# Regrouped PSUM sums, a stage-wide matmul order and one more pair in two stages of a trunk kernel

## The chip, the cores and the metric

The kernel runs on one core of a Trainium2 chip. The metric is the device time in microseconds, the median of several runs. The engines are TensorE (PE, with weight loads shown as PEld), VectorE (DVE), ScalarE (ACT), GpSimd (POOL) and SyncE (SP), which here only issues transfers.

## The reference

One layer of a streaming encoder on 1024 tokens of width 1024, all in float32:

```
h = rmsnorm(x) ; u = h @ w_in            # columns for three mixers, and 3 x 1024 gate columns
y_hg, y_ml, y_mb = HGRN2, mLSTM and Mamba-2 scans over chunks of u
gates = sigmoid(gate columns)
mixed = sum_b gates[b] * (y_b @ w_br_b) ; x = x + mixed @ w_out
u = conv3(rmsnorm(x) @ w_up) ; x = x + (silu(u_g) * u_v) @ w_down      # 2 x 2816 up columns
out = rmsnorm(x)
```

The change touches two projections: the 24 blocks of 128 gate columns, and the 44 blocks of 128 up columns, taken in 22 twos f (a block of u_g and the block of u_v beside it).

## The kernel before

Activations lie transposed: 128 channels on the partitions, 1024 tokens along the free axis. Every float32 operand is split into a high part (a cast to the matmul's format, ACT, L99) and a low part (the remainder, DVE, L100), and a product is hi\*hi + hi\*lo + lo\*hi. A plain block of 128 columns is thus 8 pieces of the contraction x 3 products x 2 token halves = 48 matmuls of 128x512 (`steps`, L136), and two blocks are 96.

Most gate and up blocks are done two at a time, with seven half-size products instead of eight (`pair_gemm` and `seven`): the contraction is halved, the tokens are halved, and some operands are sums or differences. Each of the seven is 12 matmuls (`product`, L171), so a pair is 84. Four PSUM sums take part. x is written four times, always adding to what it holds; y, z and v once each. The order is x, y, x, z, x, v, x. After each of the first three writings of x, ACT copies it out (`keep`, L188); DVE adds y, z and v to these copies (`add`, L183); at the end ACT copies x once more (L192).

PSUM has two pools. `pg` has two buffers of 1024 floats per partition (two banks each), named ps_g; `pm` has four of 512 floats, named ps_m. A plain block uses one ps_g. Before the change a pair has x and y as the two halves of one ps_g, and z and v in two ps_m. A tile is the unit on which the framework sets dependences and hands out buffers.

A pair's weights are prepared in `operands`: two raw blocks are loaded by SP (four buffers, w_raw, shared with all other weights and with the branches' y tiles), split into wa (the first block), qb (named w_b), and, after four differences in place on DVE (L160), s12 and s34 (named w_s). wa and s12 use the two buffers w_hi and w_lo that plain weights use too. This work has a higher priority with the planner than its place in the program.

The token side, `sums`, makes four differences t1 to t4 of quarters of the activations (DVE, L221) and splits them (L99, L100), once at the start of each of the two stages. The pool `a1`, which holds a pair's w_b, w_s, c and u, is opened where the sums' inputs lay, so its first use waits until these have been read.

The order of instructions on each engine is found at build time by a planner that simulates the program and takes, per engine, the ready instruction with the highest priority. `manual_schedule` fixes the written order of the named engines inside its block; instructions of other blocks can still come between. Before the change each pair is a block of its own.

The two stages: four plain gates (GATES), then the `sums`, eight gate pairs (blocks 4 to 19), four plain gates (20 to 23), and the branches, which load, cast and split the eight y tiles of a mixer (L870) and multiply. Later, f=0 of the up projection, plain f=1 and f=2 (range(1, PLAIN)), during which the `sums` are made on DVE and ACT, and 19 pairs f=3 to 21; each pair is followed by two convolutions (`up_conv`, L601 and L605), a SiLU and a product (L958, L959), and a store. Then the down projection: its first group needs two stored activations, and x2, which is fetched into the place that the t tiles leave (L241), and adds on DVE (L1001).

Of the kernel before, what the change touches and what calls it, by code (L numbers as in the profile page):

```python
# [9 lines left out]
F32 = mybir.dt.float32  # L10
# [8 lines left out]
P = 128  # L19
# [3 lines left out]
HALF = 512  # L23
# [24 lines left out]
class Trunk:  # L48
# [125 lines left out]
    def pair_gemm(self, pool, srcs, outs):  # L174

        nc = self.nc
        wa, s12, s34, qb = self.operands(pool, srcs)
        ps = self.pg.tile([P, T], F32, name="ps_g")
        x, y = ps[:, 0:HALF], ps[:, HALF:]
        z, v = (self.pm.tile([P, HALF], F32, name="ps_m") for _ in range(2))  # L180
        oa, ob = outs
        tmp = lambda: pool.tile([P, HALF], F32, name="u", bufs=4)
        add = lambda out, p, q: nc.vector.tensor_tensor(out=out, in0=p, in1=q, op=ALU.add)  # L183
        u = []

        def keep():
            u.append(tmp())
            nc.scalar.copy(out=u[-1], in_=x)  # L188

        with self.tc.manual_schedule(engines={mybir.EngineType.PE}):  # L190
            self.seven(wa, s12, s34, qb, (x, y, z, v), u, keep, add, oa, ob)
        nc.scalar.copy(out=ob[:, 0:HALF], in_=x)  # L192

    def seven(self, wa, s12, s34, qb, banks, u, keep, add, oa, ob):
        b11, b21, b22, t1, t2, t3, t4 = self.bs
# [645 lines left out]
            self.keep(self.gate_d[i], g)  # L841

    def gate_pairs(self, pool, some):
        for i in some:
            cs = [pool.tile([P, T], F32, name="c", bufs=3) for _ in range(2)]
            self.pair_gemm(pool, [self.ins["w_gate"][i + j] for j in range(2)], cs)
            for j in range(2):
                self.gate_end(i + j, cs[j])
# [120 lines left out]
            self.act(f, us)  # L969

    def up_pairs(self, pool, fs):
        for f in fs:
            ns = (2 * f, 2 * f + 1)
            cs = [pool.tile([P, T], F32, name="c", bufs=3) for _ in ns]
            self.pair_gemm(pool, [self.ins["w_up"][n] for n in ns], cs)
            us = []
            for n, c in zip(ns, cs):
                us.append(self.gp.tile([P, T], F32, name="gate", bufs=3))
                self.up_conv(us[-1], c, n)
            self.act(f, us)  # L980
# [49 lines left out]


GATES = 4
PLAIN = 3
FF_GROUPS = [(0, 2)] + [(4 * g + 2, 4) for g in range(5)]


# [106 lines left out]
def build(tc, ins, outs, dbg=None):  # L1143
    stages = dbg or dict(hg=8, ml=4, mb=4, rest=True)
    left = dict(side="left", reuse_waits="tile")
    right = dict(side="right", reuse_waits="tile")
    with ExitStack() as ctx:
        t = Trunk(tc, ctx, ins, outs, dbg)
        t.y_dram = [outs[f"y{i}"] for i in range(3)] if dbg else [
            t.dr.tile([KT, P, T], F32, name=f"y_dram{i}") for i in range(3)]  # L1150
        t.h_d = t.dr.tile([2, P, KT, HALF], F32, name="h_dram")
        t.gate_d = t.dr.tile([24, P, T], F32, name="gate_dram")
        t.x2_d = t.dr.tile([KT, P, T], F32, name="x2_dram")
        t.act_d = t.dr.tile([22, P, T], F32, name="act_dram")
        with tc.tile_pool(name="gp", bufs=3, **right) as t.gp:
            with tc.tile_pool(name="hp", bufs=1, **right) as hp:
                with ExitStack() as ms:
                    late = ms.enter_context(tc.tile_pool(name="late", bufs=1, **right))
                    early = lambda: Mix(ms.enter_context(tc.tile_pool(name="early", bufs=1, **right)), late)
                    mp, begun, v = t.first(hp, early)  # L1160
                    t.late_consts(late)
                    t.hg_setup()
                    for hd in range(stages["hg"]):
                        if hd and hd % 2 == 0:
                            v = t.hg_v(mp, hd // 2)
                        t.hg_head(mp, hd, v, begun if hd == 0 else None)
                        if hd == 5:
                            t.scalars(mp)
                    for hd in range(stages["ml"]):
                        t.ml_head(mp, hd)  # L1170
                    for g in range(stages["mb"]):
                        t.mb_group(mp, g)
                if not stages["rest"]:
                    return
                t.gates(range(GATES))
                with tc.tile_pool(name="tp", bufs=1, **right) as tp:
                    with tc.tile_pool(name="hx", bufs=2, **left) as hx:
                        xs = [hx.tile([P, KT, HALF], F32, name="h_x") for _ in range(2)]
                        for ks, hf in itertools.product((slice(0, KT // 2), slice(KT // 2, KT)), range(2)):
                            t.fetch(xs[hf][:, ks], t.h_d[hf][:, ks])  # L1180
                        quarter = lambda hf, k0: [[t.h[hf][part][:, k0 + k] for k in range(KT // 2)] for part in range(2)]
                        t.bs = [quarter(0, 0), quarter(0, KT // 2), quarter(1, KT // 2)] + t.sums(tp, xs)
                    with tc.tile_pool(name="a1", bufs=1, **left) as pool:
                        t.gate_pairs(pool, range(GATES, 24 - GATES, 2))
                t.gates(range(24 - GATES, 24))
                yp = ctx.enter_context(tc.tile_pool(name="yp", bufs=KT, **left))
                xps = ExitStack()
                xp = xps.enter_context(tc.tile_pool(name="x2", bufs=2, **left))
                br = t.branches(yp, xp)
                mixed = next(br)  # L1190
            with tc.tile_pool(name="mx", bufs=KT, **right) as mxp:
                mix = [t.pair(mxp, mixed[j]) for j in range(KT - 2)]
                for _ in br:
                    pass
                mix += [t.pair(mxp, mixed[j]) for j in range(KT - 2, KT)]
                x2 = [xp.tile([P, KT, HALF], F32, name="x2") for _ in range(2)]

                hs = [[[], []] for _ in range(4)]
                for n, part, e in itertools.product((1, 0, 2, 3), range(2), ("p_hi", "p_lo")):
                    w = yp.tile([P, T], F32R, name=e, align_bytes=ALIGN, bufs=KT)  # L1200
                    hs[n][e == "p_lo"] += [w[:, 0:HALF], w[:, HALF:]]
                place = lambda part, kt, hf: hs[kt // 4 * 2 + hf][part][kt % 4]
                rhs = lambda part, kt, ts: place(part, kt, ts.start // HALF)
                tmp = t.halves_of(lambda: t.gp.tile([P, T], F32, name="gate", bufs=3))
                src = [lambda kt, hf=hf: x2[hf][:, kt] for hf in range(2)]
                sums = lambda hf: t.norm_sums(tmp, src[hf], slice(0, HALF))


                def norm2(dg, hf):
                    t.norm(src[hf], dg, src[hf], "norm2_g",  # L1210
                           lambda kt, a: t.split(place(0, kt, hf), place(1, kt, hf), a))
                t.out_proj(mix, x2, 0, range(KT))
                t.out_proj(mix, x2, 1, [0])
                dg = sums(0)
                t.out_proj(mix, x2, 1, [1])
                norm2(dg, 0)
                t.out_proj(mix, x2, 1, range(2, KT))
            begun = t.up_begin(rhs)
            dg = sums(1)
            with tc.tile_pool(name="tp", bufs=1, **right) as tp:  # L1220
                ws, done = t.up_end(*begun, lambda: norm2(dg, 1))
                t.up_plain(range(1, PLAIN), rhs, ws)
                with tc.issue_after(done.ins):
                    t.bs = [hs[0], hs[2], hs[3]] + t.sums(tp, x2)
                xps.close()
                with tc.tile_pool(name="a1", bufs=1, **left) as pool:
                    t.up_pairs(pool, range(PLAIN, 22))
            with tc.tile_pool(name="dn", bufs=1, **right) as pool:
                t.down(yp, pool)
# [15 lines left out]
```

## Time and profile before

| | us |
|---|---|
| median of 3 runs (2536.49 to 2537.75) | 2537.37 |
| the profiled execution: its own time | 2535.01 |
| its span, first to last instruction | 2533.2 |

The span is what the profile shows. Its rows give, for a group of instructions, the busy time, the count and the mean length; a bracket at the end of a row gives the idle time of the engine before it and what ended that. A matmul's length (0.39 us) holds its way through the array, and the next starts before it ends, so distances between starts tell the pace. With a mean granted clock of 0.995 the core ran almost all of the span at the full clock. DVE was busy for 59% of the span and ACT for 40%.

### The profile page before, as it was taken

To read this page: it belongs to the slowest core of one execution; us is meant where nothing else is said; L and a number is where in the kernel's file an instruction comes from. 1 tells how busy PE (TensorE), PEld (TensorE's weight loads), DVE (VectorE), ACT (ScalarE), POOL (GpSimd) and SP (SyncE) were. 2 spreads that over 40 slices of the span, in tenths; PEclk is the share of its full clock that TensorE was granted. 3 is DMA by queue.
4 is the path that set the end of the run, shared out by engine and by line. 5 is a ranking of instruction groups with operands and counts; after the bars stand their busy time and mean duration, and the time that the engine had idled before them with its cause. 6 is when DMAs were issued, how large, how long until landed. Compare 5 with 4: busy or idle time off the path is not lost.

```text
span 2533.2 us, 31151 instructions
## 1 busy us (share of the span) xinstructions
PE 2474.8 (98%) x12980; PEld 2111.6 (83%) x12980; DVE 1503.5 (59%) x1888; ACT 1003.5 (40%) x1233; POOL 62.2 (2%) x99
## 2 busy tenths in 40 slices
PE   8999999999999999999999999999999999999998
PEld 6898989898898898899877888888777777778886
DVE  6676767774344366766844324444687777775445
ACT  5444445553334255446433312212344444441112
POOL 2000000000000000000000000000000000000000
PEclk8999999999999999999999999999999999999999
DMA  5111111111111122122323444444222222244321
GB/s 215 34 41 44 42 42 34 53 59 58 67 67 60 49 92 80 61 69 92 150 100 105 162 134 156 156 135 150 100 76 82 75 75 77 82 136 147 108 75 67
DMA packets 64141, 228.63 MB, mean 90 GB/s; under 512 B 7400, under 2 KB 8040, under 8 KB 63232
## 3 DMA queue, kind: packets, MB, share of 16 engines
q1 hardware_dynamic: 52352, 181.54, 21.6%
q0 software_dynamic: 11648, 45.09, 4.5%
q8 instruction: 102, 1.67, 0.3%
q14 instruction: 39, 0.32, 0.0%
HBM read 177.23 MB, written 49.38 MB: 89 GB/s over the span
## 4 chain that ended last, share of the span: by engine, by line
PE 94%; DVE 2%; ACT 2%; issue 1%; DMA 1%; POOL 0%; DVEq 0%; ACTq 0%
PE ps_g L136 48%; PE ps_g L171 14%; PE ps_g L270 10%; PE ps_m L171 6%; PE ps_m L136 5%; PE ps_m L464 3%; PE ps_m L797 1%; ACT w_hi L99 1%; PE ps_m L270 1%; PE ps_m L473 1%; PE ps_m L708 1%; PE ps_m L679 1%; PE ps_m L483 1%; PE ps_m L436 0%; PE ps_m L659 0%
## 5 line engine op out<-in xcount | busy, mean ns | idle before, releaser
L136 PE MATMUL ps_g<-h,w_hi 128*128 128x512 f32 x2080 | 585.0, 397 | 5.9 <-DVE h L100 3.9
L99 ACT CAST w_hi<-w_raw 128x1024 fp32r<-128x1024 f32 x209 | 218.6, 1046 | 720.4 <-PE ps_g L136 540.6
L136 PEld LDWEIGHTS ps_g<-h,w_hi 128*128 128x128 f32 x2080 | 387.7, 188 | 86.0 <-DVE h L100 4.7
L100 DVE TENSOR_TENSOR w_lo<-w_raw,w_hi 128x1024 fp32r<-128x1024 f32 x209 | 255.1, 1221 | 169.7 <-ACT w_hi L99 168.4
L136 PE MATMUL ps_g<-h,w_lo 128*128 128x512 f32 x1040 | 331.9, 395 | 0.0
L270 PE MATMUL ps_g<-w_hi,h 128*128 128x256 f32 x1408 | 261.0, 284 | 0.0
L136 PE MATMUL ps_g<-p_hi,w_hi 128*128 128x512 f32 x768 | 239.9, 390 | 5.0 <-ACT w_hi L99 2.1
L136 PE MATMUL ps_g<-p_lo,w_hi 128*128 128x512 f32 x768 | 239.2, 389 | 0.8 <-DVE p_lo L100 0.8
L136 PE MATMUL ps_g<-p_hi,w_lo 128*128 128x512 f32 x768 | 239.3, 389 | 0.0
L136 PEld LDWEIGHTS ps_g<-h,w_lo 128*128 128x128 f32 x1040 | 195.4, 188 | 40.2
L270 PEld LDWEIGHTS ps_g<-w_hi,h 128*128 128x128 f32 x1408 | 221.2, 192 | 0.6
L270 PE MATMUL ps_g<-w_lo,h 128*128 128x256 f32 x704 | 200.1, 284 | 0.0
L136 PEld LDWEIGHTS ps_g<-p_hi,w_hi 128*128 128x128 f32 x768 | 143.8, 188 | 36.9 <-ACT w_hi L99 3.4
L136 PEld LDWEIGHTS ps_g<-p_lo,w_hi 128*128 128x128 f32 x768 | 144.1, 188 | 31.3 <-DVE p_lo L100 1.1
L136 PEld LDWEIGHTS ps_g<-p_hi,w_lo 128*128 128x128 f32 x768 | 144.1, 188 | 30.1 <-DVE w_lo L100 0.3
L270 PEld LDWEIGHTS ps_g<-w_lo,h 128*128 128x128 f32 x704 | 134.9, 192 | 0.5
L188 ACT COPY u<-ps_g 128x512 f32<-128x512 f32 x81 | 45.8, 589 | 188.6 <-PE ps_g L171 186.0
L183 DVE TENSOR_TENSOR c<-ps_m,u 128x512 f32<-128x512 f32 x54 | 37.4, 692 | 129.5 <-ACT u L188 92.9
L1001 DVE TENSOR_TENSOR x<-ps_g,x 128x1024 f32<-128x1024 f32 x40 | 49.0, 1225 | 89.3 <-PE ps_g L136 88.9
L605 DVE SCALAR_TENSOR_TENSOR gate<-c,c_vec,gate 128x1023 f32<-128x1023 f32 x76 | 95.8, 1279 | 2.0 <-ACT gate L601 1.9
L100 DVE TENSOR_TENSOR p_lo<-w_raw,p_hi 128x1024 fp32r<-128x1024 f32 x48 | 58.3, 1224 | 43.5 <-ACT p_hi L99 42.8
L99 ACT CAST p_hi<-w_raw 128x1024 fp32r<-128x1024 f32 x48 | 50.4, 1050 | 84.3 <-DMA w_raw<-act_dram 30.4
(311 smaller groups left out, 4068.8 us busy)
## 6 DMA issues: line engine op xcount, KB each, us to landing
w_raw<-w_up SPq DMA_DIRECT2D x44, 512.0 KB, 3.3
w_raw<-w_hg SPq DMA_DIRECT2D x24, 512.0 KB, 3.3
w_raw<-w_v SPq DMA_DIRECT2D x24, 512.0 KB, 3.4
ta<-rows SPq DMA_DIRECT2D x24, 512.0 KB, 4.4
w_raw<-w_gate SPq DMA_DIRECT2D x24, 512.0 KB, 3.5
w_raw<-w_br SPq DMA_DIRECT2D x24, 512.0 KB, 3.8
w_raw<-y_dram SPq DMA_DIRECT2D x24, 512.0 KB, 4.4
gate<-gate_dram SPq DMA_DIRECT2D x24, 512.0 KB, 4.4
```

The source lines that it names most:

```text
L99: self.nc.scalar.copy(out=hi, in_=src)
L100: (eng or self.nc.vector).tensor_tensor(out=lo, in0=src, in1=hi.bitcast(F32), op=ALU.subtract)
L136: self.nc.tensor.matmul(out=out, lhsT=w[:, ks], rhs=rhs(part, kt, ts), start=kt == 0 and w is hi and part == 0, stop=kt == kts - 1 and w i ...
L171: self.nc.tensor.matmul(out=out, lhsT=w[x][:, ks], rhs=b[y][k], start=start and k == i == 0, stop=stop and k == 3 and i == 2, skip_group_c ...
L183: add = lambda out, p, q: nc.vector.tensor_tensor(out=out, in0=p, in1=q, op=ALU.add)
L188: nc.scalar.copy(out=u[-1], in_=x)
L270: self.nc.tensor.matmul(out=out, lhsT=self.h[hf][part][:, 4 * i + k, o:o + P], rhs=w[:, ks], start=start and k == 0 and w is hi and part = ...
L464: nc.tensor.matmul(out=pa[0:m, c], lhsT=z[:, c * P:c * P + m], rhs=part(1)[:, c], start=True, stop=True)
L473: nc.tensor.matmul(out=pa[:, j], lhsT=c3(k)[:, c + j], rhs=qs[:, c + j], start=True, stop=True)
L483: nc.tensor.matmul(out=po[:, j], lhsT=A[:, c], rhs=v[:, c, vs], start=True, stop=c == 0)
L605: end = nc.vector.scalar_tensor_tensor(out=out[:, a:ts.stop], in0=ps[:, a - d:ts.stop - d], scalar=w(d), in1=out[:, a:ts.stop], op0=ALU.mu ...
L1001: nc.vector.tensor_tensor(out=x2[j], in0=ps, in1=x2[j], op=ALU.add)
```

## The change

Three things. The four sums of a pair are regrouped: y and v are now the two halves of the ps_g, and x and z have a ps_m each. The written order of the matmuls, which held inside a pair, now holds over all pairs of a stage: the block is opened once around the loop (`in_order` is a generator that yields the jobs inside the block). And PLAIN is 2 instead of 3 and the gate pairs run to block 21 instead of 19, so there are 20 up pairs and 9 gate pairs, and one plain f (f=1) behind f=0 and two plain gates (22, 23) behind the gate pairs.

```diff
-        x, y = ps[:, 0:HALF], ps[:, HALF:]
-        z, v = (self.pm.tile([P, HALF], F32, name="ps_m") for _ in range(2))
+        y, v = ps[:, 0:HALF], ps[:, HALF:]
+        x, z = (self.pm.tile([P, HALF], F32, name="ps_m") for _ in range(2))
...
+        self.seven(wa, s12, s34, qb, (x, y, z, v), u, keep, add, oa, ob)
+        nc.scalar.copy(out=ob[:, 0:HALF], in_=x)
+
+    def in_order(self, jobs):
+
         with self.tc.manual_schedule(engines={mybir.EngineType.PE}):
-            self.seven(wa, s12, s34, qb, (x, y, z, v), u, keep, add, oa, ob)
-        nc.scalar.copy(out=ob[:, 0:HALF], in_=x)
+            yield from jobs
...
-        for i in some:
+        for i in self.in_order(some):
...
-        for f in fs:
+        for f in self.in_order(fs):
...
-PLAIN = 3
+PLAIN = 2
...
-                        t.gate_pairs(pool, range(GATES, 24 - GATES, 2))
-                t.gates(range(24 - GATES, 24))
+                        t.gate_pairs(pool, range(GATES, 22, 2))
+                t.gates(range(22, 24))
```

## Rows read from the trace of the kernel before

**Rows 1.** The page, parts 1 and 4: engines, and the chain that ended last.

```profile
PE 2474.8 (98%) x12980; PEld 2111.6 (83%) x12980; DVE 1503.5 (59%) x1888; ACT 1003.5 (40%) x1233; POOL 62.2 (2%) x99
...
PE 94%; DVE 2%; ACT 2%; issue 1%; DMA 1%; POOL 0%; DVEq 0%; ACTq 0%
```

**Rows 2.** PE's waits: waiter, waited for, us in total, times, longest.

```profile
PE ps_g L171 <- ACT w_hi L99: 17.4, 18, 1.9
PE ps_g L171 <- DVE c L183: 6.4, 8, 0.9
```

**Rows 3.** PE's timeline, gate pairs: start, length, engine, line, operation, count [idle].

```profile
1258.58 0.73 PE L171 MATMUL ps_g<-h,w_hi 128*128 128x512 f32 x2 [0.68 <-ACT u L188]
...
1270.80 2.88 PE L171 MATMUL ps_g<-t,w_s 128*128 128x512 f32 x12
1273.52 2.88 PE L171 MATMUL ps_m<-h,w_s 128*128 128x512 f32 x12
...
1282.62 0.72 PE L171 MATMUL ps_g<-t,w_hi 128*128 128x512 f32 x2 [0.78 <-DVE c L183]
...
1302.76 0.72 PE L171 MATMUL ps_g<-t,w_hi 128*128 128x512 f32 x2 [0.78 <-DVE c L183]
```

**Rows 4.** PE's timeline, up pairs: the first and last of 16 like holes.

```profile
1910.78 0.50 PE L171 MATMUL ps_g<-p_hi,w_hi 128*128 128x512 f32 x1 [0.91 <-ACT w_hi L99]
...
2217.10 0.50 PE L171 MATMUL ps_g<-p_hi,w_hi 128*128 128x512 f32 x1 [0.91 <-ACT w_hi L99]
```

**Rows 5.** Stretches: gate pairs; up pairs; 15 periods of these. Columns stand first.

```profile
core 0: us, PE busy (x) PEld busy (x) DVE busy (x) ACT busy (x) POOL busy (x), PEclk, DMA share, GB/s
1255.02:1421.91 166.89, 159.77 (x694) 129.34 (x693) 79.02 (x96) 63.97 (x80) 8.53 (x16) 1.00 0.31 107
1883.09:2276.44 393.35, 373.27 (x1609) 298.83 (x1607) 291.89 (x322) 179.29 (x211) 10.13 (x19) 1.00 0.25 87
1910.78:2217.10 306.32, 292.68 (x1261) 234.16 (x1261) 228.82 (x256) 139.26 (x166) 8.00 (x15) 1.00 0.22 78
```

**Rows 6.** PE's timeline: f=2's first matmul; behind the up pairs, two waits.

```profile
1861.33 0.39 PE L136 MATMUL ps_g<-p_hi,w_hi 128*128 128x512 f32 x1
...
2277.28 0.73 PE L136 MATMUL ps_g<-p_hi,w_hi 128*128 128x512 f32 x2 [0.68 <-ACT c L192]
...
2281.91 0.73 PE L136 MATMUL ps_g<-p_hi,w_hi 128*128 128x512 f32 x2 [1.61 <-DVE x L1001]
```

**Rows 7.** Timelines of DVE and ACT at the start of the gate pairs.

```profile
1249.66 5.76 DVE L100 TENSOR_TENSOR t<-h_x,t 128x1024 fp32r<-128x1024 f32 x5
...
1259.80 1.23 DVE L100 TENSOR_TENSOR w_lo<-w_raw,w_hi 128x1024 fp32r<-128x1024 f32 x1 [0.39 <-ACT w_hi L99]
...
1256.14 1.13 ACT L99 CAST w_b<-w_raw 128x512 fp32r<-128x512 f32 x2
...
1258.72 1.05 ACT L99 CAST w_hi<-w_raw 128x1024 fp32r<-128x1024 f32 x1 [0.19 <-DVE w_raw L160]
```

**Rows 8.** Timelines of DVE and ACT during f=1 and f=2.

```profile
1860.96 5.76 DVE L100 TENSOR_TENSOR t<-x,t 128x1024 fp32r<-128x1024 f32 x5
...
1867.77 1.28 DVE L605 SCALAR_TENSOR_TENSOR gate<-ps_g,c_vec,gate 128x1023 f32<-128x1023 f32 x1
...
1866.75 0.62 ACT L99 CAST w_b<-w_raw 128x512 fp32r<-128x512 f32 x1 [2.52 <-DVE t L100]
```

**Rows 9.** Stretches of the kernel's start, columns as in Rows 5.

```profile
12.60:18.20 5.60, 2.08 (x2) 0.50 (x2) 5.22 (x9) 5.37 (x10) 0.00 (x0) 0.50 1.02 418
...
23.40:26.20 2.80, 2.77 (x7) 2.19 (x8) 2.80 (x5) 1.53 (x3) 2.80 (x1) 0.50 0.88 374
```

**Rows 10.** The y tiles: the last split (DVE), the first cast (ACT); the chain.

```profile
1450.13 2.36 DVE L100 TENSOR_TENSOR p_lo<-w_raw,p_hi 128x1024 fp32r<-128x1024 f32 x2 [1.54 <-ACT p_hi L99]
...
1426.85 1.05 ACT L99 CAST p_hi<-w_raw 128x1024 fp32r<-128x1024 f32 x1 [3.22 <-DMA gate_dram<-c]
...
1421.91 53.27 PE ps_g L136 x235
```

**Rows 11.** Costliest groups of 1905 to 2235 us: busy, mean ns | idle before.

```profile
L183 DVE TENSOR_TENSOR c<-ps_m,u 128x512 f32<-128x512 f32 x32 | 22.1, 692 | 77.5 <-ACT u L188 56.4 <-PE ps_m L171 21.1
```

## The prediction

> **What bounds the kernel now.** I read the page first. TensorE (PE) is busy for 98% of the span and makes 94% of the chain that ended last [rows 1], so only less PE work, or fewer holes between matmuls, can move the time. Next came PE's waits: the two long entries are both on line L171, the pairs' products, and wait for L99 (a weight's split) and L183 (the DVE add that empties a sum) [rows 2]. PE's timeline shows the size. A product is 12 matmuls and takes 2.72 us (1270.80 to 1273.52), 0.2267 us a matmul; a pair is seven, 19.04 us. But gate pairs repeat every 20.14 us (1282.62 to 1302.76) [rows 3], and up pairs every 20.42 us (1910.78 to 2217.10 is 15 periods) [rows 4].
>
> The stretches give the whole loss. The gate pairs: 166.89 us for 694 matmuls; 694 x 0.2267 = 157.3, so 9.6 us are holes. The up pairs: 393.35 us for 1609 matmuls = 364.7, so 28.6 us. The granted clock is 1.00 in both [rows 5]: the holes are waits, not a slower clock. Behind the up pairs two more waits stand in the first matmuls of the down projection, 0.68 and 1.61 us idle [rows 6]; with the pipeline's restart (a wait of 0.78 us lengthens the period by 20.14 - 19.04 = 1.10 us, about 0.3 more) that is 2.9 us.
>
> **The change, part by part.**
>
> *Regrouping the sums.* In the tile of before, x and y are halves of one ps_g. The first gate pair shows what that does: y's first matmul, which needs nothing of x, starts at 1258.58 after a wait for ACT's copy of x (L188). In later pairs the next matmul into x (1282.62) waits for DVE's add that reads y (L183) [rows 3]. Each is a dependence on the tile, not on the numbers. In the up pairs the hole is entered by two matmuls of the next pair's x, which wait for that pair's weight (L99) [rows 4], and behind them x again waits for the add. With x in a tile of its own, the copy of x runs beside y's 2.72 us, the copies before the third and fourth writing of x beside z and v, and the add reading y has x, z and x, 8.2 us, before v writes the shared tile. Copy and add take under 0.7 us each plus the signal, so all fit. Next late: nothing on PE up to a pair's operands. The next pair's wa gets its buffer when y ends and is needed five products, 13.6 us, later; cast and remainder cost 1.05 + 1.23 us [rows 7].
>
> The Trainium skill says that accesses of two engines have to be kept apart by PSUM bank and quadrant (PSUM — Partial Sum Buffer, "PSUM bank collisions raise a hardware error"). x and y are 512 floats each, a bank apiece, so by that rule the wait at 1258.58 needn't be there, and a regrouping would return none of the 9.6 and 28.6 us. The row has the wait; I go by the row, and the rule's outcome is the second rival.
>
> *The stage-wide order.* It removes the running ahead into the next pair's x, which only filled holes, and the down projection's 12 matmuls inside the last pair, which then come behind it; neither adds a matmul. DVE must keep up at 19.04 us a pair: it is busy for 228.82 us over 15 up pairs, 15.3 each [rows 5]. I take the removal as full in the running pairs: 9.6 and 28.6 us.
>
> *One more gate pair, one more up pair.* A plain pair is 96 matmuls, the new one 84: 12 x 0.2267 = 2.72 us each, 5.4 us together. Each moves a border.
>
> *Start of the gate pairs (not moved).* The t sums end at 1249.66 + 5.76 = 1255.4; then follow the cast of w_b, the differences on L160 and the split of s12, whose low part ends at 1259.80 + 1.23 = 1261.0 [rows 7]: 5.6 us of chain. The pairs' buffers lie where the sums' inputs lay, so it cannot start earlier. x's second product would now be ready at 1255.02 + 5.44 = 1260.5 and needs the low part 0.45 us later: a wait of 0.1 us. I charge 0.3.
>
> *Start of the up pairs (moved 21.76 us earlier).* f=1 ends on PE at 1861.33 [rows 6]; there the pairs now begin, and x's second product is due at 1861.33 + 5.44 = 1866.8. But the t splits on DVE end at 1860.96 + 5.76 = 1866.7, and ACT's cast of w_b waits 2.52 us for just that [rows 8]. In before f=2 covers what follows. Now two L160 differences (about 1.3 us) move ahead of the sums' end, and the chain of 5.6 us comes behind: 1866.7 + 1.3 + 5.6 = 1873.6, against a need at 1866.8 + 0.45: 6.4 us of waiting. At the least it is the chain less the 0.45, 5.1; f=1's convolution (L605, at 1867.77 in before [rows 8]) may stand between with two instructions of 1.28, so at most 9. I take 6.5, nearest the gate start's order.
>
> A PE that stands that long may lose its clock. In the kernel's first stretch, with 2.08 us of matmul in 5.60, the granted clock is 0.50 (1.2 of 2.4 GHz), and the dense stretch behind it, 23.40 to 26.20, still runs at 0.50 with 7 matmuls where 12 would fit, 1.2 us lost [rows 9]. I charge 1.5, so 8.0 for this border; bounds 5 and 12. The Trainium skill states it the same way against this change: the lower clock is what an idle TensorE falls back to (TensorE: Matmul & The Clock Gate, "Part 1: The HAM clock gate"); by it the charge is due, without it the sum would be 1.5 us lower. No wait in the middle of before's span is long enough to show it.
>
> *End of the gate pairs.* The y tiles for the branches can be cast only when the last pair's buffers are stored (1426.85, 5 us behind the last product's end at 1421.91) and the last was split at 1450.13 + 2.36 = 1452.5, 30.6 us behind it [rows 10]. Two plain gates cover 21.76 us; the branches take one y each 1.36 us, so the eighth is due after 21.76 + 9.5 = 31.3. It just fits even at before's pace; that pace came from weight buffers held by the third and fourth gate, which are gone. I take 0; bounds 0 and 10 us (a third of that chain late).
>
> *End of the up pairs.* The down projection begins with free sums and early weights, so the first wait goes; the second (DVE's add at L1001 needs x2, fetched only when the pairs' t tiles are free) stays in part: 0.8 of 2.9 us.
>
> **The sum**, against the profiled execution (2535.0 us): -9.6 + 0.3 (gates) - 28.6 + 8.0 (ups) - 2.9 + 0.8 (end) - 5.4 (fewer matmuls) = -37.4, so 2497.6. The median of before's runs, 2537.4, lies 2.4 above that execution: **2500 us**. With the bounds of the borders (5 to 12 us at the start, 0 to 10 at the gates' end) and up to 5 us of small holes left in 29 pairs, the forecast's own range is 2494 to 2510.
>
> **The rivals.**
>
> 1. *DVE becomes the bound of the up pairs.* Over some 16 pairs its adds at L183 stood 77.5 us waiting for ACT's copies and PE's sums, 4.8 a pair [rows 11]; with 15.3 busy that is 20.1. If these waits don't shrink, each of 20 up pairs takes 20.1, not 19.04: +21 us, 2521. For: a strict order on DVE. Against: the waits are for PE's products, which come sooner. 10%.
> 2. *It doesn't do what it says*: the waits are not of the tile and stay, and the run-ahead that filled part of them is lost. What is left is -5.4 + 8.0, 2540. Against: rows 3, and z, in a tile of its own, shows no such wait. 3%.
> 3. *Slower: the hand-over between pairs.* Before had the next x begun inside the pair. If ACT's list has the next wa's cast behind the pair's last copy (L192), x must wait for cast and remainder at each hand-over: 1.05 + 1.23 - 0.45 = 1.8 us [rows 7]. Over 27 hand-overs that is 49 us, 2549; it is slower than before from 21 of them. Against: the buffer is free 13.6 us earlier, and a weight's split is planned ahead of other work. 4%.
> 4. *The y loads are late* by 10 us at the gates' end: 2510. 6%.
> 5. *Everything goes*, the borders too: -46, 2491. 2%.
>
> **How the numbers follow.** Forecast 75%, rivals as given. A difference under 0.2% (5 us) can't be told from none. Faster: 75 + 10 + 6 + 2 = 93%; within 0.2%: 3% (rival 2); slower: 4% (rival 3). The range for 8 in 10 goes from the clean case, 2490, over the late y loads to just short of a wholly DVE-bound stage: 2520. It leaves out rivals 2 and 3 and half of rival 1.
>
> **What would show it.** Right: matmuls 0.23 us apart through a pair, periods of 19.0 us in both stages, no wait of L171 for L183; one hole of 5 to 9 us in the first up pair, at x's second product, that ends on the split of s12 (L99, L100), perhaps with a low clock behind it; no hole where the branches begin. Wrong: periods above 19.5 us; holes at each pair's first matmul; PE idle before the first product on y; a total above 2520.

## The result, and the profile after

The changed kernel takes 2503.51 us (median of 4 runs, 2502.63 to 2505.61) against 2537.36: a ratio of 0.9868, 95% interval 0.9851 to 0.9885, so 33.9 us less. The forecast was 2500, with a range of 2490 to 2520. The profiled execution of after took 2505.61 us, the longest of its four; that of before took 2535.01. The pair of traces thus shows 29.4 us of the gain.

The page, parts 1 and 4, answers to [rows 1]: 24 matmuls fewer, 11 us less PE busy time, and PE still 94% of the chain.

```profile
PE 2463.8 (98%) x12956; PEld 2114.9 (84%) x12956; DVE 1522.5 (61%) x1908; ACT 1013.4 (40%) x1245; POOL 62.2 (2%) x99
...
PE 94%; DVE 3%; issue 1%; ACT 1%; DMA 0%; DVEq 0%; SPq 0%; ACTq 0%
```

PE's waits, after (waiter, waited for, us, times, longest). The 18 waits for ACT's w_hi and the 8 for DVE's c [rows 2] are gone. What remains on L171 is three waits in the first pairs of the two stages; behind the up pairs stands one of 2.2 us.

```profile
PE ps_m L171 <- ACT w_hi L99: 6.9, 1, 6.9
...
PE ps_g L136 <- DVE x L1005: 2.2, 1, 2.2
PE ps_m L171 <- DVE w_lo L100: 2.1, 2, 1.5
```

Stretches, after (columns as in [rows 5]): most of the gate pairs, the up pairs, and 17 periods of these. By 0.2267 us a matmul the first holds 1.6 us of holes (171.14 - 748 x 0.2267), where before had 9.6. In the third PE is busy for all of 323.36 us, and a period is 323.36 / 17 = 19.02 us against 20.42 before.

```profile
1256.06:1427.20 171.14, 169.61 (x748) 140.17 (x747) 87.67 (x107) 71.76 (x89) 9.06 (x17) 1.00 0.36 114
1851.59:2245.08 393.49, 386.02 (x1694) 318.67 (x1692) 323.82 (x352) 193.29 (x226) 10.67 (x20) 0.99 0.27 91
1899.64:2223.00 323.36, 323.36 (x1428) 267.78 (x1427) 266.17 (x292) 161.13 (x189) 9.06 (x17) 1.00 0.25 87
```

PE's timeline of the gate pairs, after; [rows 3] is its counterpart. The one hole stands in the first pair's second writing of x (1263.65). Behind it the products start 2.72 us apart, and y's first matmul comes every 19.04 us with no wait in front (1279.66 to 1298.70).

```profile
1263.65 0.50 PE L171 MATMUL ps_m<-t,w_lo 128*128 128x512 f32 x1 [1.53 <-DVE w_lo L100]
...
1268.78 2.88 PE L171 MATMUL ps_m<-t,w_s 128*128 128x512 f32 x12
1271.50 2.88 PE L171 MATMUL ps_g<-h,w_s 128*128 128x512 f32 x12
...
1279.66 0.62 PE L171 MATMUL ps_g<-h,w_hi 128*128 128x512 f32 x2
...
1298.70 0.62 PE L171 MATMUL ps_g<-h,w_hi 128*128 128x512 f32 x2
```

DVE's timeline at that hole. The add of y is issued first and stands 1.32 us for y's product; s12's low part, which PE needs, is queued behind it. In before the low part had gone first, at 1259.80 [rows 7].

```profile
1261.78 0.69 DVE L183 TENSOR_TENSOR c<-ps_g,u 128x512 f32<-128x512 f32 x1 [1.32 <-PE ps_g L171]
1262.38 2.35 DVE L100 TENSOR_TENSOR w_lo<-w_raw,w_hi 128x1024 fp32r<-128x1024 f32 x2
```

PE's timeline at the start of the up pairs, after: a wait of 6.90 us at x's second product, and a shorter one for the low part.

```profile
1856.80 0.39 PE L171 MATMUL ps_g<-p_hi,w_lo 128*128 128x512 f32 x1
1864.09 1.22 PE L171 MATMUL ps_m<-t,w_hi 128*128 128x512 f32 x2 [6.90 <-ACT w_hi L99]
1865.89 0.79 PE L171 MATMUL ps_m<-t,w_lo 128*128 128x512 f32 x1 [0.57 <-DVE w_lo L100]
...
1869.02 0.62 PE L171 MATMUL ps_m<-t,w_hi 128*128 128x512 f32 x2
```

ACT's and DVE's timelines there. DVE's last t split runs from 1855.82; ACT's w_b waits 4.20 us for it, and the cast of s12 (w_hi, 1862.99) waits 3.16 us for DVE's difference (1862.27), which comes only after two convolutions, two remainders and an add.

```profile
1858.21 0.62 ACT L99 CAST w_b<-w_raw 128x512 fp32r<-128x512 f32 x1 [4.20 <-DVE t L100]
...
1862.99 1.99 ACT L99 CAST w_hi<-w_raw 128x1024 fp32r<-128x1024 f32 x2 [3.16 <-DVE w_raw L160]
```

```profile
1855.82 2.36 DVE L100 TENSOR_TENSOR t<-x,t 128x1024 fp32r<-128x1024 f32 x2
1858.09 1.28 DVE L609 SCALAR_TENSOR_TENSOR gate<-ps_g,c_vec,gate 128x1023 f32<-128x1023 f32 x1
...
1862.27 0.69 DVE L160 TENSOR_TENSOR w_raw<-w_raw 128x512 f32<-128x512 f32 x1
```

PE's, then the load queue's and DVE's timelines at the end of the up pairs. The answer to [rows 6]: the first of the two waits is gone, the second is 2.18 us, and the matmuls behind it stand 0.43 us apart for a while.

```profile
2240.54 0.61 PE L136 MATMUL ps_g<-p_hi,w_lo 128*128 128x512 f32 x2
...
2242.36 2.88 PE L171 MATMUL ps_m<-t,w_b 128*128 128x512 f32 x12
2245.08 0.62 PE L136 MATMUL ps_g<-p_hi,w_hi 128*128 128x512 f32 x2
...
2250.14 0.73 PE L136 MATMUL ps_g<-p_hi,w_hi 128*128 128x512 f32 x2 [2.18 <-DVE x L1005]
...
2252.80 1.05 PE L136 MATMUL ps_g<-p_lo,w_hi 128*128 128x512 f32 x2
...
2255.05 0.63 PE L136 MATMUL ps_g<-p_lo,w_hi 128*128 128x512 f32 x2
```

```profile
2245.27 3.99 SPq L245 DMA_DIRECT2D x<-x_dram  x8
```

```profile
2248.86 1.22 DVE L1005 TENSOR_TENSOR x<-ps_g,x 128x1024 f32<-128x1024 f32 x1 [3.51 <-DMA x<-x_dram]
```

At the gates' end, DVE's last y split and the chain, to be held against [rows 10]: the split ends at 1454.4, 20.5 us behind the last product (1433.95), where before needed 30.6. The branches wait for nothing.

```profile
1453.21 1.23 DVE L100 TENSOR_TENSOR p_lo<-w_raw,p_hi 128x1024 fp32r<-128x1024 f32 x1 [1.78 <-ACT p_hi L99]
```

```profile
1433.95 38.08 PE ps_g L136 x168
```

DVE's adds in 17 up periods (1900 to 2220 us), to be held against [rows 11]: 22.5 + 13.6 + 13.5 = 49.6 us of standing, 2.9 a pair instead of 4.8.

```profile
L183 DVE TENSOR_TENSOR c<-ps_g,u 128x512 f32<-128x512 f32 x33 | 22.7, 688 | 22.5 <-PE ps_g L171 22.5
...
L183 DVE TENSOR_TENSOR u<-ps_m,u 128x512 f32<-128x512 f32 x17 | 11.8, 692 | 13.6 <-PE ps_m L171 13.6
L183 DVE TENSOR_TENSOR c<-ps_m,u 128x512 f32<-128x512 f32 x17 | 11.8, 691 | 13.5 <-ACT u L188 13.5
```

### The profile page after: what moved, and what is told of

Read it like the earlier page. It is cut to its first block, busy times and chain, and to the rows that moved or that the text cites. A ratio compares the mean times of both kernels' runs of the same rounds, so it can differ in the third digit from the quotient of the medians.

```text
span 2503.8 us, 31125 instructions
## 1 busy us (share of the span) xinstructions
PE 2463.8 (98%) x12956; PEld 2114.9 (84%) x12956; DVE 1522.5 (61%) x1908; ACT 1013.4 (40%) x1245; POOL 62.2 (2%) x99
## 4 chain that ended last, share of the span: by engine, by line
PE 94%; DVE 3%; issue 1%; ACT 1%; DMA 0%; DVEq 0%; SPq 0%; ACTq 0%
PE ps_g L136 46%; PE ps_m L171 16%; PE ps_g L274 10%; PE ps_g L171 6%; PE ps_m L136 5%; PE ps_m L468 3%; PE ps_m L801 1%; PE ps_m L274 1%; PE ps_m L477 1%; PE ps_m L712 1%; PE ps_m L683 1%; PE ps_m L487 1%; PE ps_m L440 0%; PE ps_m L663 0%; PE ps_m L685 0%
## 5 line engine op out<-in xcount | busy, mean ns | idle before, releaser
L136 PE MATMUL ps_g<-h,w_hi 128*128 128x512 f32 x2016 | 568.6, 398 | 5.8 <-DVE h L100 3.9
L136 PEld LDWEIGHTS ps_g<-h,w_hi 128*128 128x128 f32 x2016 | 376.3, 189 | 83.1 <-DVE h L100 4.7
L136 PE MATMUL ps_g<-h,w_lo 128*128 128x512 f32 x1008 | 322.5, 396 | 0.0
L136 PE MATMUL ps_g<-p_hi,w_hi 128*128 128x512 f32 x736 | 230.3, 391 | 2.8 <-DVE x L1005 2.2
L136 PE MATMUL ps_g<-p_lo,w_hi 128*128 128x512 f32 x736 | 229.9, 390 | 0.8 <-DVE p_lo L100 0.8
L136 PE MATMUL ps_g<-p_hi,w_lo 128*128 128x512 f32 x736 | 230.1, 391 | 0.0
L136 PEld LDWEIGHTS ps_g<-h,w_lo 128*128 128x128 f32 x1008 | 189.8, 189 | 39.1
L136 PEld LDWEIGHTS ps_g<-p_hi,w_hi 128*128 128x128 f32 x736 | 138.5, 188 | 32.9 <-DVE x L1005 2.6
L136 PEld LDWEIGHTS ps_g<-p_lo,w_hi 128*128 128x128 f32 x736 | 138.4, 188 | 30.2 <-DVE p_lo L100 1.1
L136 PEld LDWEIGHTS ps_g<-p_hi,w_lo 128*128 128x128 f32 x736 | 138.4, 188 | 29.0 <-DVE w_lo L100 0.3
L171 PE MATMUL ps_m<-t,w_hi 128*128 128x512 f32 x464 | 144.4, 392 | 6.9 <-ACT w_hi L99 6.9
L171 PEld LDWEIGHTS ps_m<-t,w_hi 128*128 128x128 f32 x464 | 87.9, 190 | 25.6 <-ACT w_hi L99 7.3
L1005 DVE TENSOR_TENSOR x<-ps_g,x 128x1024 f32<-128x1024 f32 x40 | 49.0, 1225 | 91.6 <-PE ps_g L136 87.9
L188 ACT COPY u<-ps_m 128x512 f32<-128x512 f32 x87 | 51.1, 588 | 127.3 <-PE ps_m L171 127.3
L171 PE MATMUL ps_m<-t,w_lo 128*128 128x512 f32 x232 | 91.2, 393 | 2.1 <-DVE w_lo L100 2.1
```

Source lines behind the costliest of these rows:

```text
L136: self.nc.tensor.matmul(out=out, lhsT=w[:, ks], rhs=rhs(part, kt, ts), start=kt == 0 and w is hi and part == 0, stop=kt == kts - 1 and w i ...
L171: self.nc.tensor.matmul(out=out, lhsT=w[x][:, ks], rhs=b[y][k], start=start and k == i == 0, stop=stop and k == 3 and i == 2, skip_group_c ...
L1005: nc.vector.tensor_tensor(out=x2[j], in0=ps, in1=x2[j], op=ALU.add)
```

## The experiments

Each median is set against runs of before on the same chip. The first four take the change apart; the others test its borders.

### Regrouping alone (e4_regroup_alone)

Before, with only the sums regrouped: order inside each pair, PLAIN 3, eight gate pairs.

```diff
-        x, y = ps[:, 0:HALF], ps[:, HALF:]
-        z, v = (self.pm.tile([P, HALF], F32, name="ps_m") for _ in range(2))
+        y, v = ps[:, 0:HALF], ps[:, HALF:]
+        x, z = (self.pm.tile([P, HALF], F32, name="ps_m") for _ in range(2))
```

> The kernel before with the regrouping alone (y and v share the ps_g, x and z have a ps_m each); the order stays one block per pair, PLAIN 3, 8 gate pairs. Theory (the sharing of x and y made the holes): the 9.6 and 28.6 us of holes go but for about 1.8 at the gates' start: 2537.4 - 36.4 = 2501 us, periods of 19.0 us. Rival (the order over the whole stage is needed, since the planner would still run ahead into the next pair's x and wait for its weight): holes of about 1 us per pair stay, 2525 to 2537 us.

Measured: 2499.49 us, ratio 0.9853 (0.9838 to 0.9868): 36 us less, as expected. The whole change gave 34, and the intervals of the two ratios overlap, so the medians alone don't show that the regrouping by itself is better. Of PE's waits on L171 in it one is left, the first gate pair's.

```profile
PE ps_m L171 <- DVE w_lo L100: 1.5, 1, 1.5
```

The holes came from the grouping, and the regrouping alone removes them.

### The order alone (e5_order_alone)

Before, with the block opened once around each stage (`in_order`) and nothing else.

```diff
-        for i in some:
+        for i in self.in_order(some):
...
-        for f in fs:
+        for f in self.in_order(fs):
```

> The kernel before with the stage-wide order alone; x and y share the ps_g as before, PLAIN 3, 8 gate pairs. Theory (the run-ahead only filled the holes that the shared tile makes): y waits for ACT's copy of x and x for DVE's add in each pair, 0.9 + 1.1 = 2.0 us in 27 pairs, 54 us against 38 before: 2537.4 + 16 = 2553 us, slower than before. Rival (the order itself removes the holes): 2505 us or less.

Measured: 2556.03 us, ratio 1.0077 (1.0060 to 1.0094), 20 us slower, where 16 were expected. PE's waits of this kernel:

```profile
PE ps_g L171 <- ACT u L188: 20.8, 27, 2.3
PE ps_g L171 <- DVE c L183: 20.1, 25, 0.9
```

Nearly each of the 27 pairs now has both waits, 40.9 us in all, where before had 17.4 + 6.4 [rows 2]. What the planner drew forward in before had filled a part of the holes. With the regrouping there is nothing left to fill: the step from e4 to e1 (below) is this order and one gate pair, and its ratio moves by 0.0011, 2.8 us, of which a gate pair is 2.7. That is no more than either ratio's interval is wide, so the times leave room for a few us either way; the lists of waits show none.

### Which halves share the tile (e3_xv_shared)

After, with x beside v instead of y beside v.

```diff
-        y, v = ps[:, 0:HALF], ps[:, HALF:]
-        x, z = (self.pm.tile([P, HALF], F32, name="ps_m") for _ in range(2))
+        x, v = ps[:, 0:HALF], ps[:, HALF:]
+        y, z = (self.pm.tile([P, HALF], F32, name="ps_m") for _ in range(2))
```

> The changed kernel with other partners: x and v are the halves of the ps_g, y and z have a ps_m each; order, counts and PLAIN as changed. Theory (a dependence is set on the tile, though the halves lie in different PSUM banks): v must wait for ACT's copy of x just before it (about 0.9 us, as y did at 1258.58 before), and x's last product for DVE's add that reads v (about 1.1 us, as at 1282.62): 2.0 us in each of 29 pairs, 58 us, 2561 us, with PE L171 waiting for L183 and for L188. Rival (dependences by bank; the holes went through the stage-wide order): no new holes, 2503.5 us.

Measured: 2561.08 us (two runs), ratio 1.0093 (1.0073 to 1.0113). PE's waits:

```profile
PE ps_g L171 <- DVE c L183: 22.0, 28, 0.8
PE ps_g L171 <- ACT u L188: 18.2, 27, 0.7
```

The same number of tiles and banks, 58 us more than after. v and the fourth writing of x stand next to each other in the order, so v waits for the copy of x, and x for the add that reads v, once a pair. PE's timeline shows both places inside one up pair: v's first matmul, and behind v the first of x's last product. The waits stand between neighbours of one pair, not at the hand-over of a buffer to the next pair.

```profile
1956.01 0.50 PE L171 MATMUL ps_g<-p_hi,w_s 128*128 128x512 f32 x1 [0.68 <-ACT u L188]
...
1959.82 3.04 PE L171 MATMUL ps_g<-t,w_b 128*128 128x512 f32 x12 [0.78 <-DVE c L183]
```

It is not the number of tiles that counts but that neighbours in the order are in different ones.

### The counts alone (e6_counts_alone)

Before, with PLAIN 2 and nine gate pairs only.

```diff
-PLAIN = 3
+PLAIN = 2
...
-                        t.gate_pairs(pool, range(GATES, 24 - GATES, 2))
-                t.gates(range(24 - GATES, 24))
+                        t.gate_pairs(pool, range(GATES, 22, 2))
+                t.gates(range(22, 24))
```

> The kernel before with the counts alone: PLAIN 2 and 9 gate pairs, x and y sharing the ps_g, one block per pair. Theory (the two extra pairs save 12 matmuls each but have the holes of their stage, 1.1 and 1.4 us, and the first up pair waits for its s12 as after the whole change): -5.4 + 2.5 + 9 = +6, 2543 us, or some 3 less where the planner runs ahead into the second pair's x and fills part of the wait. Rival (the earlier start costs nothing in the old order, since the run-ahead fills the wait): 2534.5 us.

Measured: 2540.76 us, ratio 1.0012 (1.0003 to 1.0022). 24 matmuls fewer (5.4 us) and yet 3.2 us slower: about 8.6 us are given back. Of these 2.5 are the two more pairs' own holes, so some 6 are left for the borders, where 9 were expected, or 6 with the run-ahead. The wait at the up pairs' start is another than the expectation named: y's first matmul stands for ACT's copy of x, not x's product for s12.

```profile
1868.61 0.80 PE L171 MATMUL ps_g<-p_hi,w_hi 128*128 128x512 f32 x1 [4.32 <-ACT u L188]
```

Behind it 7 matmuls start 0.43 us apart. The trace is of the slowest of ten executions and has more such stretches behind the last pairs' waits, so the 6 us is not the price of this one border alone.

### Each count by itself (e1_plain3, e2_gates20)

After with PLAIN 3, and after with eight gate pairs and four plain gates.

```diff
-PLAIN = 2
+PLAIN = 3
```

> The changed kernel with PLAIN back at 3: two plain f behind f=0, 19 up pairs; all else as changed (9 gate pairs). Theory (the hole of 6.9 us idle in the first up pair, with the half clock behind it, 9.9 us in all, stands there because the sums end too late for the earlier start): the hole goes, and a pair becomes plain again, so 2503.5 - 9.9 + 2.7 = 2496.3 us, PE never idle for over 1 us in L171 during the up pairs, clock 1.00 there. Rival (the hole comes from the stage-wide order or the regrouping, not from the earlier start): the hole stays, 2503.5 + 2.7 = 2506 us.

```diff
-                        t.gate_pairs(pool, range(GATES, 22, 2))
-                t.gates(range(22, 24))
+                        t.gate_pairs(pool, range(GATES, 20, 2))
+                t.gates(range(20, 24))
```

> The changed kernel with the gate pairs ending at block 19 again: 8 gate pairs, four plain gates behind them; PLAIN stays 2. Theory (the extra gate pair costs nothing at its border, as the y tiles are in time): only the 12 matmuls come back, 2503.5 + 2.7 = 2506.2 us. Rival (the border with two plain gates costs something that no wait shows, such as slower transfers): 2503.5 or less.

Measured: 2497.18 us (0.9842, 0.9827 to 0.9856) and 2506.70 us (0.9879, 0.9864 to 0.9894). So the twentieth up pair costs 6.3 us in balance: every run of e1 (2496.50 to 2498.14) lies below every run of after. The ninth gate pair gains about 3 by the medians, as its 12 matmuls would; but the intervals of after and e2 overlap, so this gain is in keeping with the expectation and not shown by itself. In e1 the hole at the up pairs' start is gone, since f=2 covers the chain again; the wait behind the up pairs is there still:

```profile
PE ps_g L136 <- DVE x L1005: 2.1, 1, 2.1
```

### A shorter chain for the first up pair (e7_far_first)

After; in the first up pair s12 is made in a third raw buffer and split before qb.

```diff
-            for out, x, y, op in ((a1, a1, b1, ALU.subtract), (b1, b1, b2, ALU.add), (b2, b2, a1, ALU.subtract),
-                                  (a2, a2, b2, ALU.subtract)):
+            far = self.wr.tile([P, 1024], F32, name="w_raw") if first else raw[1]
+            c1, c2 = far[:, 0:HALF], far[:, HALF:]
+            for out, x, y, op in ((a1, a1, b1, ALU.subtract), (c1, b1, b2, ALU.add), (c2, b2, a1, ALU.subtract),
+                                  (a2, a2, c2, ALU.subtract)):
...
+            self.split(*s12, far)
+            if first:
+                qb = new("w_b", HALF, 4)
+                self.split(*qb, b2)
```

> The changed kernel, but the first up pair alone writes b1+b2 and b2-a1 into a third raw buffer instead of in place, and splits s12 from there before qb: s12 no longer waits for w_b's buffer, which lies where the sums' inputs lie. Theory (the hole is the chain sums' end, cast of w_b, differences, split of s12): s12 is split before the sums end; what still waits for them is ACT's copy of x into u, about 1.5 us after, so the hole falls from 6.9 us idle to 2.5 or less and the clock does not fall: 2503.5 - 9.9 + 2.5 = 2496 us. Rival (DVE is simply late with all its work there, wherever the buffers lie): the hole stays within 1 us of 6.9, 2503 us.

Measured: 2499.89 us, ratio 0.9850 (0.9834 to 0.9867): 3.6 less than after and 3.9 more than forecast. PE's wait in that place (the product's line is L178 here, the copy's L195):

```profile
PE ps_m L178 <- ACT u L195: 3.4, 1, 3.4
```

The expectation was half right. The chain of s12 did set the 6.90 us, but the wait behind it, which the expectation put at 2.5 us or less, came out at 3.4. ACT's copy of x goes into a buffer of the pool `a1`, which opens with the last read of the sums' inputs, and on ACT it also stood behind three casts (from 1857.32; the copy starts at 1859.74). How much of the 3.4 us is the pool and how much is ACT's queue isn't separated. This standing was again followed by the lower clock, which had not been expected.

### x2 early, and a shorter chain in the gates (e8_early_x2, e9_far_gate)

e8 is e1 with x2's first tile in a free buffer of `a1`, so that its load needn't wait for the t tiles; e9 is e8 with e7's third raw buffer in the first gate pair.

```diff
-                        x2.append(pool.tile([P, T], F32, name="x2", bufs=KT))
+                        x2.append(pool.tile([P, T], F32, name="x2", bufs=KT) if j else x20)
...
+                x20 = pool.tile([P, T], F32, name="c", bufs=3)
```

> The version with PLAIN 3 and 9 gate pairs (2497.2 us), and x2's first tile in the down projection takes a c buffer of the pairs' pool, which is free before the last pair ends, not one that the t tiles leave; the pool stays open. Theory (the wait of 2.1 us behind the up pairs, and 1.7 us of half clock behind it, come from the fetch of x2's first tile, which starts only when the last product has read its t tile): both go, 2497.2 - 4.1 = 2493.1 us. Rival (the wait is DVE's, which still has the last pair's convolutions in its queue before the add): at most 1 us of it goes, 2496 us or more.

```diff
-            self.pair_gemm(pool, [self.ins["w_gate"][i + j] for j in range(2)], cs)
+            self.pair_gemm(pool, [self.ins["w_gate"][i + j] for j in range(2)], cs, i == GATES)
```

> The same with, besides, the third raw buffer for s12 in the first gate pair (as was tried in the first up pair). Theory (the hole of 1.5 us idle in the first gate pair is s12's low part, queued on DVE behind the add that reads y): s12 is split earlier and the hole goes: 1.7 us less than the version without it, 2491.4 us. Rival (the copy of x into u, whose place also waits for the sums, or DVE's queue takes its place): no change within 0.7 us.

Measured: 2494.14 us (0.9827, 0.9812 to 0.9841) and 2492.34 us (0.9820, 0.9805 to 0.9835). Both are about 1 us above what was expected. The steps of 3.0 and 1.8 us are within the intervals of the ratios; that each wait went is read from the traces. In e9's list no wait of the products is left, and this is all that stands behind the up pairs (L1012 is after's L1005):

```profile
PE ps_g L136 <- DVE x L1012: 0.2, 1, 0.2
```

In e8 PE's list has no wait there at all, and its timeline shows the full pace behind the last pair: from the first of these rows to the second there are 42 starts in 9.52 us, 0.2267 each.

```profile
2237.11 0.61 PE L136 MATMUL ps_g<-p_hi,w_hi 128*128 128x512 f32 x2
...
2246.63 0.61 PE L136 MATMUL ps_g<-p_hi,w_hi 128*128 128x512 f32 x2
```

e9 is the best version seen: 45 us below before, and 11 below after.

## Why the prediction was right, step by step

**The running pairs.** All of the holes were forecast to go, and all went: periods of 19.02 to 19.04 us, no wait for L183 or L188. e4 shows that the regrouping did it, e3 and e5 that the waits return when x shares a tile with its neighbour in the order. That is also the answer to rival 2 and to the Trainium skill's rule (PSUM — Partial Sum Buffer, "PSUM bank collisions raise a hardware error"): in e3 x and v are 512 floats each in one tile, and PE stands 40.2 us for the other half's reader. What waits is the tile; the rule on banks tells of collisions, not of such waits. One of the holes that the 28.6 us took in was of another kind: inside the last pair, among the down projection's matmuls, PE stood for a weight. It is gone in e4 and in after.

```profile
2259.95 0.74 PE L136 MATMUL ps_g<-p_hi,w_hi 128*128 128x512 f32 x2 [2.06 <-ACT w_hi L99]
```

**The order.** Forecast to add no matmul and to put the down projection's 12 matmuls behind the last pair. It didn't: matmuls of L136 stand inside that pair in after too (2240.54). As the order changed nothing measurable beside the regrouping, this cost nothing.

**Fewer matmuls.** 24, by the page; 5.4 us.

**Start of the gate pairs.** Charged 0.3, measured 1.8: the wait of 1.53 and its restart (12 matmuls from 1261.51 to 1266.06 take 4.55 us, where 2.72 is the full pace). The term took DVE's order from before, where the low part of s12 went ahead of the add of y. With the regrouping y begins 2.72 us behind the pairs' start instead of 3.56, and the planner put the add first; so the add's wait for y's product became the low part's wait. Why the planner chose so isn't shown. e9, with that low part made earlier, loses the hole and 1.8 us.

**Start of the up pairs.** Charged 8.0 (6.5 of standing, 1.5 of clock). From 1856.80 to 1869.02 there are 10 starts, 2.27 us by the full pace, so 9.95 us were lost: 7.5 in the two waits, the rest at the lower clock and in the restart. Place, cause and kind were right, the size was 1.9 short, about 1 in the standing and 1 behind it: between the t splits and the difference DVE also had two convolutions, two remainders and an add.

**End of the gate pairs.** Charged nothing, and nothing was lost; the y tiles came in 20.5 us, faster than the 30.6 that the bounds were made from.

**End of the up pairs.** Here the term failed: charged 0.8, measured 4.1. The prediction took the two waits of before for a sum of which one goes. But both stood beside the same chain: x2's load is issued when the t tiles have been read for the last time, and its add ends about 5 us later. This row of before has the issue; from it to the second wait's end at 2281.91 [rows 6] it is 5.3 us, and in after from 2245.27 to 2250.14 it is 4.9.

```profile
2276.63 4.60 SPq L241 DMA_DIRECT2D x<-x_dram  x8
```

The first wait had hidden a part of that chain. In before the profile puts the add's own wait down to PE's product, which the first wait had made late; in after it puts it down to the load (3.51 us, above). So in before the two came out nearly together:

```profile
2280.63 1.23 DVE L1001 TENSOR_TENSOR x<-ps_g,x 128x1024 f32<-128x1024 f32 x1 [0.80 <-PE ps_g L136]
```

Between the pair's end (2245.08 in after) and the restart stand 12 matmuls, 2.72 us, and 2.34 us of loss. The other 1.7 us is the clock: 14 matmuls from 2250.14 to 2255.05 took 4.91 us where 3.17 is the full pace. e8, which lets the load start early, removes the standing and the slow stretch. The standing belongs to the change; the slow stretch need not come with it, for e2 has the same wait, 2.21 us, without it (last section).

**The sum.** Forecast for the profiled execution 2497.6, measured 2505.6, 8.0 more: gates 1.5, ups 1.9, end 3.3, and 1.1 for a slower start of the kernel that has nothing to do with the change; 0.2 stays open. That the median lies only 3.5 above the forecast is luck: the profiled execution is 2.1 above after's median, and that of before was 2.4 below its own. All three border terms were too small, 9.1 us charged together and 15.9 measured; the terms for the running pairs and the matmuls carry the forecast. The prediction's own range, 2494 to 2510, does not follow from its bounds either: 5 to 12 and 0 to 10 us at the borders and 5 of small holes give 2497 to 2519.

**The rivals.** 1 (DVE-bound): DVE is busy 266.17 / 17 = 15.7 us a pair, stands 2.9 for the sums, and the period stays 19.0. 3 (late hand-over): no wait at any pair but the first. 4 (late y loads): none. 5 (everything goes): not with this change; e9, at 2492.3, comes near its 2491, with PLAIN 3 and two more edits.

**What the prediction had and did not draw.** By its own terms the twentieth up pair gains 2.7 and costs 8.0. The sum was forecast as one change; as three it says: regroup, keep PLAIN 3. That is e1, 6.3 us faster than the change as made.

## What to carry to other kernels

Where an accumulator is read out between its writings, put what stands next to it in the order into another tile, even where the halves are different banks: here that was worth 36 us, and the wrong partner cost 58. Two waits in a row on one engine are not a sum to be taken off one by one: look for the chain that runs beside both, for removing the first may only lengthen the second. When one more block moves a border, charge the border in the same line as the block's gain, and count DVE's whole queue in it, not the chain alone.

## What the runs showed of the hardware

A stand of 2.18 us in the middle of a dense run was followed by a lower granted clock in after, which the standing of before (0.68 and 1.61 us a few matmuls apart, [rows 6]) was not. The stretch behind the up pairs, and that at their start, after (columns as in [rows 5]):

```profile
1862.14:1868.97 6.83, 4.30 (x9) 2.98 (x10) 6.79 (x9) 2.94 (x3) 0.54 (x1) 0.50 0.47 153
2251.26:2254.67 3.41, 3.41 (x10) 2.63 (x9) 2.34 (x3) 0.00 (x0) 0.00 (x0) 0.50 1.02 412
```

At 0.50 (1.2 of 2.4 GHz) a matmul takes 0.43 us. In the second stretch PE is busy throughout, and the fall came 1.1 us after it had restarted, so the price of a short wait can stand behind it, where the list of waits doesn't show it. The prediction weighed this for the long stand of the up pairs alone.

The length of the stand does not settle it. In e2 PE stands 2.21 us at the same place, for the same add, restarts at 2253.16, and keeps the full clock:

```profile
2254.30:2257.60 3.30, 3.30 (x16) 2.71 (x15) 3.30 (x3) 0.00 (x0) 0.00 (x0) 1.00 1.03 412
```

Before's stands of 1.94 us (to 2238.55) and 2.06 us (to 2259.95) and e5's of 2.28 us (to 2255.39) were followed by the full clock too. e6's of 1.88 us (to 2243.14) was followed by 0.54 from 2244.30 to 2247.70, and e1's, e4's and e7's of 2.14 to 2.15 us behind the up pairs by the lower clock as in after. The stands of 3.0 us and more in the two stages of pairs, up to 6.95, were all followed by it. What decides between the shorter ones is not shown, so 1.7 us behind a stand of 2 us is a price that one execution pays and another doesn't.

The low clock at the kernel's start differs between executions of like code. In the stretch from 25.80 to 29.10 us the granted clock was 0.93 with 15 matmuls in the trace of before,

```profile
25.80:29.10 3.30, 3.30 (x15) 2.69 (x14) 3.30 (x6) 0.00 (x0) 3.30 (x1) 0.93 0.97 318
```

and 0.50 with 9 in that of after:

```profile
25.80:29.10 3.30, 3.30 (x9) 2.54 (x9) 3.30 (x6) 0.00 (x0) 3.30 (x1) 0.50 1.08 367
```

In e1 it was 0.59 and in e4 0.83. Why is not settled; it is about 1 us of what differs from run to run.
